# Rank-and-scatter kernel: twelve tiles of row copies from register loops, even groups, ranks finished by batch, a ring of four groups, an early Pool drain

## Chip, cores, metric

One core of one Trainium2 chip. The metric is the device time of one execution in microseconds (us), measured on the chip; every figure of time is a median of several executions unless it is called a span. The span is what the profiler sees, from the first to the last instruction, and is 1 to 3 us shorter than the time.

## The reference

For each of 8 batches, 2048 rows of 2560 floats (10 KB a row) are put in the order of their scores:

```python
B, N, D = 8, 2048, 2560
order = np.argsort(scores, axis=1)
ranks = np.argsort(order, axis=1)
out[b_idx, ranks, :] = x
```

So 168 MB are read and 168 MB written, and a row's place is its rank.

## The kernel before

VectorE counts, for each row, how many scores of its batch are smaller. That gives ranks. The rows are then moved in two ways.

*Bulk.* Pool loads a group (256 rows, 128 partitions x 20 KB, or 128 rows x 10 KB) into one of eight buffers and then writes each tile of 128 rows with one indirect DMA, a "scatter", to the rows that the ranks name. All of this goes through one DMA queue, q0. A load is issued only when the scatters `LAG` groups back have landed:

```python
NBUF = 8; LAG = 2; G = 16
GROUPS = [(0, 1, range(B)), (P, 1, range(3))] + [(256 * i, 2, ()) for i in range(1, 8)]
...                                             # (first row, tiles, batches done by row copy)
for k in range(1, NBUF):
    load(pl, k, s_load[k])
for k, (b, g) in enumerate(BULK):
    i = k % NBUF
    if k >= LAG and k + NBUF - LAG < len(BULK):
        scatters_done(pl, k - LAG)              # 16 increments, one per DMA engine, for each scatter
        load(pl, k + NBUF - LAG, s_load[(k - LAG) % NBUF])
    ...                                         # wait for the load of k and for its ranks
    for j in range(GROUPS[g][1]):
        scatter(k, j, 0, P, rank_i, s_scat[i][j])   # (the SPLIT branch is never taken: SPLIT is empty)
```

*Row copies.* 11 of the 128 tiles go straight from `x` to `out` without a buffer, a row at a time, from the two hardware queues of SP (q1) and ACT (q10). The loop is unrolled: 704 DMAs on each.

```python
for n, (b, g, j, q) in enumerate(todo):
    line, name = ((sp, ENG.SP), (act, ENG.Activation))[n % 2]
    ...                                         # at = 16 destination addresses loaded in registers
    for i in range(G):
        row = r + m * (G * q + i) + j
        line.eng.dma_start(
            out=out_bytes[bass.ds(at[i], ROW)],
            in_=x_bytes[b, row, :],
        ).then_inc(s_rows[line], 16)
```

At the end SP waits for the last scatters; Pool issues nothing after its last scatter.

## Time and profile before

| | before |
|---|---|
| time | 795.67 us (795.51 to 795.81, 3 runs) |
| span of the profiled run | 795.4 us |
| DMA, all 16 engines | busy in every slice, about 404 GB/s over the span |
| VectorE / PE / Pool busy | 411 / 33 / 148 us |

Read it from the DMA side: no compute engine is busy for more than about half of the span, and the DMA engines are full throughout. The page's line of busy times (us, share of the span, instructions):

```profile
PE 33.3 (4%) x155; PEld 27.2 (3%) x155; DVE 411.2 (52%) x1002; POOL 148.4 (19%) x186
```

The slices, queues and stretches are in the prediction, which works with them. The DMA row is a mean of 16 engines. Packet records carry a queue, a size and a duration.

### The profile page before, as it was taken

How to read it: one execution, taken by the hardware profiler on the slowest of the kernel's cores; microseconds unless marked ns; L12 is line 12 of the kernel's file. 1: busy time of each engine (PE TensorE's matmuls, PEld its weight loads, DVE VectorE, ACT ScalarE, POOL GpSimd, SP SyncE). 2: the span in 40 equal slices, each digit the busy share in tenths (PEclk: the TensorE clock that was granted, in tenths of full speed). 3: DMA queues.
4: the chain of work that ended last, by engine and by line, in shares of the span. 5: the costliest groups of instructions: out<-in, count | busy, mean ns of one | idle time of the engine just before them, and what ended most of it. 6: DMA issues, size and time to landing. Idle time of an engine off the chain costs nothing.

```text
span 795.4 us, 4586 instructions
## 1 busy us (share of the span) xinstructions
PE 33.3 (4%) x155; PEld 27.2 (3%) x155; DVE 411.2 (52%) x1002; POOL 148.4 (19%) x186
## 2 busy tenths in 40 slices
PE   3002010020020100200000000000000000000000
PEld 3001010010010100100000000000000000000000
DVE  6999999999999999999994000000000000000000
POOL 3102121212121212022111212122121212111600
PEclk9555555555555555555555555555555555555555
DMA  8999999999999999999999999999999999999994
GB/s 364 431 402 365 424 415 425 417 422 417 425 417 418 347 420 422 422 367 420 421 420 423 397 397 421 420 419 380 420 411 423 420 386 407 401 431 426 390 428 193
DMA packets 70737, 321.57 MB, mean 404 GB/s; under 512 B 25384, under 2 KB 47912, under 8 KB 47912
## 3 DMA queue, kind: packets, MB, share of 16 engines
q0 software_dynamic: 25488, 304.10, 91.3%
q1 hardware_dynamic: 22688, 9.94, 4.9%
q10 hardware_dynamic: 22528, 7.25, 3.9%
q14 instruction: 32, 0.26, 0.1%
q8 instruction: 1, 0.02, 0.0%
HBM read 167.84 MB, written 167.77 MB: 422 GB/s over the span
## 4 chain that ended last, share of the span: by engine, by line
DVE 47%; DMA 40%; issue 4%; POOL 3%; PE 1%; POOLq 0%; SPq 0%
DVE trash L258 41%; DMA out_dram<-x,rank_i 38%; DVE s_all L235 2%; DMA x<-in_x_dram 2%; POOL out_dram L361 2%; DVE rank L284 1%; DVE rank L290 1%; DVE rank_i L307 1%; POOL x L122 1%; DMA s_in<-in_scores_dram 0%; PE ps_all L190 0%; PE ps_col L169 0%; DVE rows_i L220 0%; POOLq L28 0%; DVE s_col L177 0%
## 5 line engine op out<-in xcount | busy, mean ns | idle before, releaser
L258 DVE TENSOR_SCALAR_CACHE_REDUCE trash<-s_all,s_col 128x1792 bf16<-128x1792 f32 (+9 forms) x248 | 315.3, 1306 | 0.3
L122 POOL DMA_DIRECT2D x<-in_x_dram x60 | 33.8, 565 | 545.8 <-DMA out_dram<-x,rank_i 376.5
L361 POOL DMA_INDIRECT out_dram<-x,rank_i x117 | 112.8, 964 | 59.0 <-issue 35.3
L258 DVE SCALAR_TENSOR_TENSOR trash<-s_all,s_col,mask 128x256 bf16<-128x256 f32 (+1 forms) x128 | 59.0, 461 | 0.0
L190 PE MATMUL ps_all<-ident,s_col 128*128 128x128 f32 x128 | 27.2, 399 | 247.4 <-DVE s_all L235 247.0
L190 PEld LDWEIGHTS ps_all<-ident,s_col 128*128 128x128 f32 x128 | 24.4, 213 | 249.4 <-DVE s_all L235 249.0
L235 DVE COPY s_all<-ps_all 128x512 f32<-128x512 f32 x32 | 20.1, 683 | 1.8 <-PE ps_all L190 1.5
L258 DVE DVE_READ_ACCUMULATOR trash<-s_all,s_col 128x1 f32 x248 | 19.9, 80 | 0.0
L290 DVE TENSOR_TENSOR rank<-rank,acc 128x2 f32<-128x2 f32 (+1 forms) x72 | 11.5, 160 | 2.5
L284 DVE TENSOR_TENSOR rank<-acc,acc 128x2 f32<-128x2 f32 (+1 forms) x72 | 11.5, 160 | 2.5
L307 DVE CAST rank_i<-rank 128x2 int32<-128x2 f32 (+1 forms) x61 | 10.7, 176 | 1.8
L258 DVE DVE_READ_ACCUMULATOR trash<-s_all,s_col,mask 128x1 f32 x128 | 10.2, 80 | 0.0
L300 PE MATMUL ps_row<-ident,rank 128*1 128x128 f32 x11 | 4.1, 372 | 101.3 <-DVE rank L290 92.7
L300 PEld LDWEIGHTS ps_row<-ident,rank 128*1 128x1 f32 x11 | 0.9, 79 | 105.0 <-DVE rank L290 95.5
L220 DVE TENSOR_SCALAR rows_i<-ps_row 1x128 int32<-1x128 f32 x11 | 3.0, 272 | 0.0
L177 DVE COPY s_col<-ps_col 128x128 f32<-128x128 f32 x1 | 0.3, 292 | 4.8 <-PE ps_col L169 4.8
L169 PE MATMUL ps_col<-ident,s_in 8*128 8x8 f32 x16 | 2.0, 261 | 4.0 <-DMA s_in<-in_scores_dram 4.0
L169 PEld LDWEIGHTS ps_col<-ident,s_in 8*128 8x128 f32 x16 | 1.9, 211 | 4.0 <-DMA s_in<-in_scores_dram 4.0
L150 POOL TENSOR_SCALAR_AFFINE_SELECT mask<-mask 128x256 f32<-128x256 f32 x2 | 0.8, 398 | 0.0
L162 DVE MEMSET acc<- 128x128 f32 x1 | 0.2, 165 | 1.1 <-SPq L98 1.1
L133 POOL MEMSET mask<- 128x512 f32 x1 | 0.5, 525 | 0.0
L132 POOL MEMSET ident<- 128x128 f32 x1 | 0.2, 204 | 0.5 <-SPq L98 0.5
(5 smaller groups left out, 0.7 us busy)
## 6 DMA issues: line engine op xcount, KB each, us to landing
x<-in_x_dram POOLq DMA_DIRECT2D x55, 2560.0 KB, 19.2
out_dram<-in_x_dram SPq DMA_DIRECT2D x704, 10.0 KB
out_dram<-in_x_dram ACTq DMA_DIRECT2D x704, 10.0 KB
x<-in_x_dram POOLq DMA_DIRECT2D x5, 1280.0 KB, 16.7
x<-in_x_dram SPq DMA_DIRECT2D x1, 2560.0 KB, 13.4
out_dram<-x,rank_i POOLq DMA_INDIRECT x117, 23.5
s_in<-in_scores_dram SPq DMA_DIRECT2D x1, 64.0 KB
```

Source lines behind the costliest of these rows:

```text
L122: line.eng.dma_start(out=xb[k % NBUF][:, :m * D], in_=x[b, r:r + P * m, :].rearrange("(p j) d -> p (j d)", j=m),).then_inc(sem, 16)
L150: nc.gpsimd.affine_select(out=part, in_=part, pattern=[[0, MMAX], [-1, P]], compare_op=OP.is_ge, fill=0.0, base=-half, channel_multiplier=1,)
L169: nc.tensor.transpose(out=ps_col[:, B * c:B * (c + 1)], in_=s_in[:, r + j:r + m * P:m], identity=ident[:B, :B],)
L190: nc.tensor.transpose(out=ps_all[:, P * c:P * (c + 1)], in_=s_col[:, c, b:b + 1].to_broadcast([P, P]), identity=ident[:],)
L220: nc.vector.tensor_scalar(out=rows_i[DIRECT.index((b, g))][:m, :], in0=ps_row[:m, :P], scalar1=float(b * N), scalar2=float(ROW), op0=OP.ad ...
L235: nc.vector.tensor_copy(out=s_all[:, 512 * q:512 * (q + 1)], in_=ps_all[:, 512 * q:512 * (q + 1)],)
L258: how.pop("do")(out=trash[i][:, :P * (hi_c - lo_c)], in0=s_all[:, P * lo_c:P * hi_c], accum_out=acc[which][:, col:col + 1], **how,)
L284: nc.vector.tensor_tensor(out=rank[:, cols], in0=acc[0][:, cols], in1=acc[1][:, cols], op=OP.add)
L290: nc.vector.tensor_tensor(out=rank[:, cols], in0=rank[:, cols], in1=acc[2][:, cols], op=OP.add)
L300: nc.tensor.transpose(out=ps_row[:m, :P], in_=rank[:, cols], identity=ident[:])
L307: nc.vector.tensor_copy(out=rank_i[:, cols], in_=rank[:, cols])
L361: nc.gpsimd.indirect_dma_start(out=out_flat, out_offset=bass.IndirectOffsetOnAxis(ap=index[:hi - lo, col:col + 1], axis=0), in_=xb[k % NBU ...
```

## The change

The intent: (1) even groups, so that every load and every group is two tiles; the first 256 rows of batches 0 to 5 are row copies, 12 tiles instead of 11; (2) the row copies as register loops, six per queue, 16 rows a pass, so that the code is short; (3) ranks of a batch finished together, fewer small VectorE instructions; (4) a ring in which a load waits for scatters four groups back instead of two; (5) a Pool drain after its last scatter, so that the runtime's own drain at the end finds nothing to do.

```diff
-    GROUPS = [(0, 1, range(B)), (P, 1, range(3))] + [(256 * i, 2, ()) for i in range(1, 8)]
+    GROUPS = [(256 * i, 2) for i in range(8)]
+    DIRECT = range(6)
...
-    LAG = 2
+    LAG = 4
...                                  # the ranks: the same counting operations, one add/add/cast
...                                  # for a batch (batch 0 in four steps) instead of one per group
+        for b in DIRECT:
+            for h, (line, name) in enumerate(((sp, ENG.SP), (act, ENG.Activation))):
+                line.after(dve, t_rows[b])
+                half = WIDE // 2
+                with line.eng.Fori(0, half // G) as q:
+                    _, at = nc.values_load_multi_w_load_instructions(
+                        rows_i[b][:, bass.ds(half * h + q * G, G)], ...
+                    for i in range(G):
+                        row = b * N + GROUPS[0][0] + half * h + i
+                        line.eng.dma_start(
+                            out=out_bytes[bass.ds(at[i], ROW)],
+                            in_=x_bytes[bass.ds(q * (G * ROW) + row * ROW, ROW)],
+                        ).then_inc(s_rows[line], 16)
...                                  # the unused SPLIT branch, rank_t, s_last go
             for j in range(GROUPS[g][1]):
+                scatter(k, j)
+        nc.gpsimd.drain()
```

## The prediction

> **What bounds the kernel now.** I read the page first (busy lines, slices, queues), then the same measures in stretches, then the packet records of the trace. Slices and queues of the page:
>
> ```profile
> DMA  8999999999999999999999999999999999999994
> GB/s 364 431 402 365 424 415 425 417 422 417 425 417 418 347 420 422 422 367 420 421 420 423 397 397 421 420 419 380 420 411 423 420 386 407 401 431 426 390 428 193
> ...
> q0 software_dynamic: 25488, 304.10, 91.3%
> q1 hardware_dynamic: 22688, 9.94, 4.9%
> q10 hardware_dynamic: 22528, 7.25, 3.9%
> q14 instruction: 32, 0.26, 0.1%
> ```
>
> The 16 DMA engines are full from the first slice to the last; the shares add up to 100%. VectorE is busy 411 us, all before 426 us, Pool 148 us. So only three things can move the time: work taken off the DMA engines, stretches in which they are busy but slow, and the two ends. The GB/s row shows the slow stretches: mostly about 420, but 347, 367, 380 now and then. The stretches:
>
> ```profile
> 75.00:259.00 184.00, 12.76 (x53) 10.22 (x53) 180.84 (x441) 32.38 (x39) 0.51 1.02 419
> 264.00:274.00 10.00, 2.18 (x10) 2.18 (x11) 9.83 (x20) 2.07 (x3) 0.50 1.05 292
> 339.00:349.00 10.00, 0.00 (x0) 0.00 (x0) 9.79 (x27) 2.49 (x3) 0.50 1.05 334
> 544.00:554.00 10.00, 0.00 (x0) 0.00 (x0) 0.00 (x0) 2.48 (x3) 0.50 1.02 350
> 734.00:744.00 10.00, 0.00 (x0) 0.00 (x0) 0.00 (x0) 6.93 (x8) 0.50 0.99 361
> 744.00:784.00 40.00, 0.00 (x0) 0.00 (x0) 0.00 (x0) 6.01 (x7) 0.50 1.00 425
> 784.00:791.00 7.00, 0.00 (x0) 0.00 (x0) 0.00 (x0) 0.00 (x0) 0.50 0.08 34
> ```
>
> The last two columns are DMA share and GB/s. 184 us run evenly at 419; then come dips of some 10 us with the engines as busy but at 292 to 388. The last line is the tail: one engine of 16 still works, alone, for about 6 us.
>
> The packet records say what the dips are. A 20 KB load packet takes 761 ns (median), a 10 KB scatter packet 385, a 640 B piece of a row copy 32 plus 9 for its completion. At these medians all packets add to (15616 x 385 + 7168 x 761 + 22528 x 41 + 2832 x 9) / 16 = 776 us per engine; the records add to 797. The 20 us between are load packets of up to 2200 ns (13 us) and row pieces (5 us), nearly all inside the dips. In the dips row pieces run at twice their usual rate per q0 packet.
>
> When do they come? Once at the start (50 to 75 us, where the first scatters follow eight loads). None from 75 to 259 us, batches 1 and 2, whose bulk groups are all two tiles. From batch 3 on each batch has one bulk group of a single tile (10 KB load packets, one scatter instead of two), and from 264 us there is a dip after nearly each such load and another where its lone scatter comes up (339, 444, 464, 544, 569, 644, 669, 734). I take the single-tile groups as the cause; the correlation is all I have.
>
> **What the skill says.** (1) "DMA: Bandwidth & Descriptors", section "Queues, rings and completion order": an engine round-robins between its queues at packet granularity. The trace agrees: from 75 to 259 us an engine took 384 q0 packets and 192 rows on each hardware queue, and a row is two packets. (2) Same page, "Where 436 GB/s comes from": a fabric ceiling of 435 GB/s. The pure scatter stretch has 425, the mix 419: nothing more is to be had there. (3) "Runtime: NRT & Kernel Launch", "Instruction fetch mechanics": instructions are streamed in 16 KiB blocks, and a taken branch outside the two-page window stalls on a fetch. The trace shows 32 packets of 8 KB on q14, about 0.31 us each; no loop is in this kernel, so it cannot show the stall.
>
> **The change, part by part.**
>
> *Twelve tiles instead of eleven by row copy.* Bulk costs (761/2 + 385)/16 = 47.6 ns of the 16 engines per row, a row copy 41. So 128 rows save 0.8 us.
>
> *All bulk groups two tiles.* The steady stretch repeats every 13.1 us per group of two tiles (load starts at 121.2, 134.3, 147.4). A period has 8 + 16 data and 3 completion packets of q0 per engine, 27, hence 27 row copies beside them. After the change there are 58 bulk groups: 58 x 13.1 = 760 us, with room for 58 x 27 = 1566 rows; 1536 are wanted. The row copies fit, with 2% to spare. The thirty missing rows give back 1.2 us. That is 758.6. The dips belonging to single-tile groups should go: 12 us by the GB/s missing in the eight stretches against 420 (3.05 + 2.05 + 0.9 + 0.9 + 1.7 + 1.2 + 1.0 + 1.4), some 17 by the spacing of the load starts there over 13.1 us per pair; the difference is row pieces served ahead, which are work too.
>
> *Register loops.* SP and ACT issue 704 rows each:
>
> ```profile
> L341 SPq MOVE out_dram<-in_x_dram x704: 29/29/38, 24.3 to 690.1; - x176
> L341 SPq DMA_DIRECT2D out_dram<-in_x_dram x704: 517/548/2704, 24.3 to 690.2; - x176
> L330 SPq TENSOR_LOAD <-rows_i x44: 967/1654/3367, 23.1 to 676.6; - x44
> ```
>
> Unhindered, one row takes 0.63 us (median spacing at the start), plus 1.75/16 = 0.11 for the load of 16 registers. After, 768 rows have from about 20 us to about 775: 0.98 us each. A source address that depends on the loop register costs perhaps two or three more register instructions of some 65 ns (the distance from MOVE to DMA), and the branch 0.03 per row: 0.63 + 0.11 + 0.16 + 0.03 = 0.93. It fits, barely. The code shrinks by about 2 x 1400 instructions of 64 bytes, some 20 of the 32 fetch packets, 6 us. That would matter little spread over 16 engines (0.4 us), but one engine ends 6 us behind the other fifteen, and 32 x 0.31 = 10 us of fetches on one engine would explain that. I credit 3 of the 6.
>
> *Ranks by batch.* Batch b's scatters wait for all its ranks: about 59 us for batch 0, 107 for batch 1 (48 us each, some 5 less than the 52 before). Pool then has three groups of batch 0 scattering and L and S packets for 46 us behind; by this estimate the ring runs dry at about 126, so 107 is early enough. Later batches are further ahead. Hidden; VectorE's saving is hidden too.
>
> *Four groups in the ring.* The wait before a load is on scatters four groups back, not two. The idle of Pool (376 us on scatters) is not on the path, since the ring never ran dry before. Worth 0, perhaps a longer pure scatter phase at the start.
>
> *Drain.* At the end the runtime's drain of Pool stands alone:
>
> ```profile
> L420 POOLq DRAIN  x3: 46/72/3015, 791.6 to 795.1; - x3
> ```
>
> 3.0 us after the last landing at 790.9. A drain put after Pool's last scatter (753 us) runs beside 38 us of transfers. If the later one then is short, 2.9 us are won; I count 2.4.
>
> *Sum.* Start 3 (the first slice's 364 GB/s against 430) + 758.6 + start dip 3 + 3 unexplained + late engine 3 + end 2 = 773. The 3 unexplained come from the same sum for the kernel before: 3 + 58.5 x 13.1 - 171 missing rows x 0.041 + 6 late engine + 4.4 end = 773; with 17 of dips and 2.3 at the start, 792 of 795.4. The other way: 795.7 - 12.2 dips - 3 late engine - 2.4 drain - 0.8 = 777. I take 775.
>
> **Rivals.** (a) The dips stay: they come from something else, such as engines drifting into step, and the deeper ring changes nothing or spreads them. For it: one dip at the start has no single-tile group. Against it: 184 us without one. Then 795.7 - 6 = 788 to 790. (b) Row issue becomes the bound: at 1.05 us per row SP would end at 20 + 806, so 826 us; loops straddling a fetch block would add to it. For it: only 2% of room; a straddling loop or a fourth register instruction is enough. Against it: my count of 0.93, and some thirty rows of buffer in each hardware queue (31 issued in the first 20 us while about 16 rows had been served). A milder form, rows ending a few us after the scatters, is likely; 2 us for it lie between my two sums. (c) Rank starvation at batch 1: an idle stretch near 110 us, at most some 10 us. (d) The drain's 3 us recur at the end: 778.
>
> **Range and chances.** The limit of 2% is 779.8. Most mixtures of half-credits lie between 768 and 789. Dips gone and rows fitting: about two chances in three, below the limit. Dips staying: about a quarter. Rows over time or starvation beyond 2%: one in twenty.
>
> **What would show it.** Right: the GB/s row even at 415 to 425 after some 90 us, the load packets' sum close to their medians, row copies ending within 15 us of the last scatter, fewer than 15 q14 packets, the last engine within 3 us of the others, and a final Pool drain under 0.1 us. Wrong: dips persisting in batches 3 to 7 with no single-tile groups; SP's and ACT's row spacing above 0.98 us with q0 empty at the end; a hole near 110 us; a final drain still of 3 us.

## The result, and the profile after

| | before | after |
|---|---|---|
| time, same rounds | 795.59 us (794.1 to 795.81, 4 runs) | 793.43 us (793.15 to 793.65, 4 runs) |
| ratio | | 0.9977 [0.9959, 0.9994]: the same |
| span of the profiled run | 795.4 | 791.4 |

A ratio here and below is the mean time of one kernel's fast runs over the mean of the other's in the same rounds, so it is not quite the ratio of the quoted medians; the bracket is its 95% interval.

The predicted 775.0 is missed by 18 us, and the range by 4. Yet most signs that the prediction had named for "right" are there. Slices and queues of the changed kernel's page:

```profile
DMA  8999999999999999999999999999999999999960
GB/s 366 423 407 416 425 416 423 418 425 415 427 414 425 415 424 416 425 420 422 419 419 421 420 422 420 422 418 423 418 424 419 422 419 423 418 425 418 417 252 19
...
q0 software_dynamic: 24912, 301.48, 89.5%
q1 hardware_dynamic: 24736, 10.60, 4.9%
q10 hardware_dynamic: 24576, 7.91, 4.0%
q14 instruction: 14, 0.11, 0.0%
```

From the fourth slice to the 38th it stays between 414 and 427 GB/s: the dips are gone. Fetch packets fell from 32 to 14. But look at the end: DMA 9, 6, 0 instead of 9, 9, 4. The same measures in stretches (width in us after the window; the last two columns are DMA share and GB/s), the dips' windows first:

```profile
75.00:259.00 184.00, 11.47 (x54) 10.17 (x54) 177.08 (x359) 0.00 (x0) 34.98 (x42) 0.51 1.02 420
264.00:274.00 10.00, 4.00 (x18) 3.52 (x18) 8.26 (x16) 0.00 (x0) 0.00 (x0) 0.67 1.02 419
339.00:349.00 10.00, 0.00 (x0) 0.00 (x0) 9.89 (x23) 0.00 (x0) 2.56 (x3) 0.50 1.05 432
544.00:554.00 10.00, 0.00 (x0) 0.00 (x0) 0.00 (x0) 0.00 (x0) 2.48 (x3) 0.50 1.02 418
764.00:786.00 22.00, 0.00 (x0) 0.00 (x0) 0.00 (x0) 0.00 (x0) 0.00 (x0) 0.50 0.07 30
```

The windows that had 292, 334 and 350 GB/s now have 419, 432 and 418. The last line is the news: for 22 us, 764 to 786 us, the DMA share is 0.07, which is one engine of sixteen, and 30 GB/s. Before, the engines were full until 784 and one worked alone for some 6 us. **Fifteen engines now finish 20 us earlier; the sixteenth finishes 4 us earlier between these two profiled runs, and it is the one that sets the end.**

The packet records show the same. Their clock runs some 10.7 us ahead of the span's. Each scatter ends with a 4-byte completion on every engine. The last completions of q0 come, in the kernel before, at 795.7, 798.7 and 801.8 us; in the changed one at 777.1, 777.6, 780.5, 783.9, 787.2, 790.6, 793.9 and 797.3 us. One per 3.3 us is what a single engine needs for its eight 10 KB packets of a scatter beside row pieces: one engine is seven scatters behind; before, it was two.

*What the slow engine does.* I followed its chain of q0 packets back from the last completion: at each step to a packet of the right size that ended just before the next began. The records have no engine number, so single links can be wrong; the sums are what I use. After the first 70 us, against the other fifteen:

| changed kernel | last engine | others | times | us |
|---|---|---|---|---|
| scatter packets, 10 KB, mean ns | 402.0 | 385.8 | 918 | 14.9 |
| load packets, 20 KB, mean ns | 764.1 | 761.3 | 400 | 1.1 |
| gaps in which row pieces are served, us | 50.5 | 43.5 | | 7.0 |
| fetch packets | 2 | 0 | | 0.6 |
| sum | | | | 23.6 |

The other engines are done at about 774, it at 797.3: the sum is the lag.

A check made afterwards divides the same sum more sharply. In this trace nearly every packet starts 3 or 4 ns before the end of the packet before it on its engine, whatever the queue, and the order of sizes in each queue is known. With both, all sixteen chains can be followed at once, and they hardly mix. After 70 us the last engine then has 919 scatter packets of 406.9 ns on average, 562 of them over 400 ns; the others have 385.4 on average, and at most 5 over 400 on any one. Its loads take 764.6 ns against 761.2, its gaps 47.0 us against 45.3. So about 20 of the 23 us are stretched scatter packets. The single chains used in the table above, and in the tables and means below, mix in some packets of other engines, so their "last" means for scatters are on the low side.

Spread over sixteen engines the work would have ended at (15 x 774 + 797.3) / 16 = 775.5 instead of 797.3, 22 us earlier: 772 us of time, an estimate from these records. So the sum in the prediction, which treats the sixteen as one pool, was close to right for the pool.

*The row copies fit.* SP's instructions of the loop (duration in ns min/median/max, then the first and last start):

```profile
L311 SPq MOVE out_dram<-in_x_dram x1536: 29/29/128, 19.8 to 759.6; - x192
L311 SPq DMA_DIRECT2D out_dram<-in_x_dram x768: 447/521/2196, 19.9 to 759.6; - x192
L311 SPq ALU_OP  x728: 32/33/55, 19.7 to 759.4; - x182
```

A register source address costs one ALU_OP of 33 ns and a second MOVE of 29 ns, 62 ns a row; the median spacing of rows inside a pass of 16 rose from 0.646 to 0.742 us. With the register load and the step to the next pass, the fastest passes take 0.84 to 0.89 us a row, below the 0.98 that the time allows.

*The drain.* The early one, and the one at the end:

```profile
L350 POOLq DRAIN  x1: 37592/37592/37592, 752.9 to 752.9; - x1
```

```profile
L379 POOLq DRAIN  x3: 34/47/72, 790.7 to 791.2; - x3
```

The longest drain at the end is 0.07 us instead of 3.0. But the early one lasts until 790.5, 3.8 us after the last landing, so the end still comes 4.7 us after the last landing (before: 4.4).

### The profile page after: what moved, and what is told of

Its sections match the earlier page's. It is cut to its first block, busy times and chain, and to the rows that moved or that the text cites. A ratio compares the mean times of both kernels' runs of the same rounds, so it can differ in the third digit from the quotient of the medians.

```text
span 791.4 us, 7991 instructions
## 1 busy us (share of the span) xinstructions
PE 30.9 (4%) x156; PEld 27.6 (3%) x156; DVE 398.3 (50%) x809; ACT 0.0 (0%) x1; POOL 146.2 (18%) x182
## 4 chain that ended last, share of the span: by engine, by line
DVE 43%; another core or an unknown queue 30%; POOL 8%; DMA 6%; issue 6%; PE 3%; POOLq 0%; SPq 0%
DVE trash L207 41%; POOL out_dram L328 6%; DMA x<-in_x_dram 6%; PE ps_all L180 2%; POOL x L112 2%; DVE s_all L279 1%; PE ps_row L254 0%; DMA s_in<-in_scores_dram 0%; PE ps_col L159 0%; DVE rank_i L245 0%; DVE rank L239 0%; DVE rank L233 0%; POOLq L350 0%; POOLq L28 0%
## 5 line engine op out<-in xcount | busy, mean ns | idle before, releaser
L207 DVE TENSOR_SCALAR_CACHE_REDUCE trash<-s_all,s_col 128x1792 bf16<-128x1792 f32 (+7 forms) x240 | 315.2, 1348 | 4.6
L112 POOL DMA_DIRECT2D x<-in_x_dram x57 | 32.1, 566 | 462.2 <-DMA out_dram<-x,rank_i 441.1
L207 DVE SCALAR_TENSOR_TENSOR trash<-s_all,s_col,mask 128x256 bf16<-128x256 f32 x128 | 61.6, 481 | 0.0
L207 DVE DVE_READ_ACCUMULATOR trash<-s_all,s_col,mask 128x1 f32 x128 | 10.7, 83 | 0.0
L264 DVE TENSOR_SCALAR rows_i<-ps_row 1x256 int32<-1x256 f32 x6 | 2.5, 411 | 4.1 <-PE ps_row L254 4.1
L245 DVE CAST rank_i<-rank 128x16 int32<-128x16 f32 (+3 forms) x11 | 2.0, 180 | 0.4
L239 DVE TENSOR_TENSOR rank<-rank,acc 128x16 f32<-128x16 f32 (+3 forms) x11 | 1.9, 170 | 0.4
L233 DVE TENSOR_TENSOR rank<-acc,acc 128x16 f32<-128x16 f32 (+3 forms) x11 | 1.9, 170 | 0.4
```

What stands on the lines that cost most here:

```text
L112: line.eng.dma_start(out=xb[k % NBUF][:, :m * D], in_=x[b, r:r + P * m, :].rearrange("(p j) d -> p (j d)", j=m),).then_inc(sem, 16)
L207: do(out=trash[i][:, :P * (hi_c - lo_c)], in0=s_all[:, P * lo_c:P * hi_c], accum_out=acc[i][:, col:col + 1], **how,)
L233: nc.vector.tensor_tensor(out=rank[:, cols], in0=acc[0][:, cols], in1=acc[1][:, cols], op=OP.add)
L239: nc.vector.tensor_tensor(out=rank[:, cols], in0=rank[:, cols], in1=acc[2][:, cols], op=OP.add)
L245: nc.vector.tensor_copy(out=rank_i[:, cols], in_=rank[:, cols])
L264: nc.vector.tensor_scalar(out=rows_i[b][:].rearrange("o (p j) -> o p j", p=P), in0=ps_row[:1, :WIDE].rearrange("o (j p) -> o p j", p=P), s ...
```

## The experiments

Theory A: the dips of the kernel before were the fifteen engines held back to the slow one by the short ring; the deeper ring lets them go, and the end is the slow engine's own chain. The code allows it: with `LAG` = 2, the load that follows group k-1's scatters in the queue is issued only after group k-2's scatters have landed on all sixteen engines. A fast engine that has finished group k-1 has nothing of q0 until then; it can be ahead by about one group (13.1 us less the issue), or half of that when the group is a single tile. With `LAG` = 4 it is three groups. Rival B is the prediction's: the dips belong to the single-tile groups themselves. Further rivals concern the slow engine: instruction fetches, the drain, the row copies.

### 1. The ring alone, in the kernel before

```diff
-    LAG = 2
+    LAG = 4
```

> The kernel before with the four-group ring alone; its single-tile groups stay. Theory A (one DMA engine of 16 is behind; a short ring holds the other fifteen back to it, which is what the dips are; its own work sets the end): the dips go, that engine ends 15 us or more behind the others, and the time stays within 1% of before (788 to 798). Rival B (the dips belong to single-tile groups, as I predicted): the dips at 264 us and after stay, and the last engine stays about 6 us behind.

Measured: 794.21 us (794.06 to 794.54) against 795.45; ratio 0.9984 [0.9967, 1.0001]. Slices:

```profile
DMA  8999999999999999999999999999999999999960
GB/s 363 432 399 415 423 416 423 417 425 414 425 417 425 418 418 423 419 420 420 419 424 418 419 420 420 426 421 417 422 417 426 421 417 422 417 426 432 427 283 20
```

All single-tile groups are still there and the dips are not. Load packets beyond their median fell from 13.4 to 2.0 us per engine. The other engines are done at about 777 (record clock), the last at 798.7: a lag of 22 us, made with one number. B falls and A stands: one changed number gives the whole picture of the changed kernel.

### 2. The short ring, in the changed kernel

```diff
-    LAG = 4
+    LAG = 2
```

> The changed kernel with two groups in the ring instead of four. Theory A: dips come back although no group has a single tile, the last engine is only some 6 us behind, and the time is about the changed kernel's, 790 to 797. Rival B: no dips, an even 420 GB/s, the lag stays above 15 us.

Measured: 792.54 us (792.39 to 792.95) against 795.45; 0.9965 [0.9948, 0.9982]. Slices:

```profile
DMA  8999999999999999999999999999999999999992
GB/s 365 426 406 399 424 416 426 415 424 418 422 416 427 416 394 417 417 404 415 415 404 410 422 419 415 418 385 426 414 415 416 416 404 410 415 420 404 421 420 80
```

The dips come back (394, 404, 404, 385, 404) with no single-tile group in the kernel, but shallower than before (347, 367, 380). Excess of the loads: 9.7 us, against 13.4 before. That fits the length of a group: single-tile groups were not the cause, but made the short ring shorter in time. The fifteen end at about 785, the last at 796.2: a lag of 11 us, where some 6 had been expected, and no later end than with the deep ring. The deep ring is worth nothing here.

### 3. No row copies

```diff
-    DIRECT = range(6)
+    DIRECT = range(0)
```

> The changed kernel without any row copy: 64 bulk groups. Theory A1 (the slow engine's scatter packets are stretched only while row copies run: 402 ns on it against 386 on the others): all scatter packets 385 ns, all engines end within 2 us, 64 x 12.2 + 8 = 788 to 791 us, so no slower than the changed kernel. Rival C (that engine is slow on scatters anyway): it ends 64 x 16 x 17 ns = 17 us behind the others and the time is 803 to 808.

Measured: 798.36 us (798.13 to 798.42) against 795.45; 1.0036 [1.0019, 1.0053]. Slices:

```profile
DMA  8999999999999999999999999999999999999994
GB/s 364 432 411 429 418 434 426 423 428 422 431 427 421 432 427 429 433 429 429 432 429 432 430 430 429 431 431 432 427 433 431 427 436 429 429 432 430 428 430 203
```

The time missed what I expected by 8 us: I had added the start and end wrongly, and some lag stays. The mechanism came out: the scatter packets of the last engine are 385.7 ns on average, the others' 385.2; 2 of 1007 are over 400. The stretching that made most of the lag is gone with the row copies. The last engine still ends at 801.6, 1.5 to 7 us behind the others (794.3 to 800.1), where 2 us had been expected, from a few long loads (771.6 against 765.4 on average) and 4 fetches.

### 4. Row copies on ten engines, first attempt

```diff
+                        if i % 3 == 0:
+                            to, of = (v.rearrange("(a b) -> a b", a=10) for v in (to, of))
```

> The changed kernel with every third row copy (6 of 16) cut into 10 pieces of 1024 bytes in place of 16 of 640, so that 576 rows use only ten engines. Theory A with the slow engine among the six left out: it is relieved of 576 x 38 ns = 22 us, the ten get 9 us more, and the end moves from 797 to about 783 in the packet records: 777 to 783 us. If the slow engine is among the ten: 798 to 806 us. If what it does is not the bound: within 1% of 793.

Measured: 793.31 us (792.61 to 793.57); 0.9970 [0.9954, 0.9987]. The edit did nothing: every row is still 16 packets of 640 B, 12288 on each queue. As a repeat of the changed kernel it shows the same lag (others 775, last 797.2; 401.5 against 386.0 ns). Inconclusive for its question.

### 5. Less bulk on one engine

Two bulk groups loaded and scattered with 120 of 128 partitions, meant to leave an engine free, their 32 left-over rows by row copy:

```diff
+    PART = {(5, 1): 120, (7, 1): 120}
...
-                out=xb[k % NBUF][:, :m * D],
+                out=xb[k % NBUF][:PART.get((b, g), P), :m * D],
```

> The changed kernel, but two of its 58 bulk groups move only 120 of 128 partitions; the 32 rows left over go by row copy. The Trainium skill says that a software-queue transfer of that height may leave out the last engine. Theory A, if the slow engine is the last one and it is left out: it is relieved of 2 x (8 x 0.76 + 16 x 0.40) = 25 us and pays 32 x 0.05 back, ends with the others at about 775 in the packet records, and the time is 769 to 776 us. If another engine is the slow one, or the transfers spread over all 16: 790 to 796 us and a lag of 20 us as now.

Measured: 824.47 us (820.29 to 825.6) against 795.35; 1.0346 [1.0317, 1.0376]. The rule that this expectation rests on is in the section of the Trainium skill that is quoted under 12 to 15. A misfire: the transfers of 120 partitions have 48 completion packets more than full ones (2816 in all instead of 2768; 24 for each of the six such transfers instead of 16, if shared evenly), and for the last 25 us of the scatters only about four packets run at once. How the transfers were spread over the engines was not established. Nothing follows for the slow engine.

### 6. Without the early drain

```diff
-        nc.gpsimd.drain()
```

> The changed kernel without the Pool drain. The trace of the changed kernel shows that drain running 37.6 us, until 3 us after the last landing. If the drain merely waits for the landings and then takes the same 3 us: ratio to before as the changed kernel's, 0.9977 within 0.0015. If it saves the final drain, as I predicted: 2.9 us (0.0036) slower than that.

Measured: 797.16 us (796.91 to 797.63) against 795.35; 1.0023 [1.0006, 1.0039]. The drain at the end:

```profile
L378 POOLq DRAIN  x3: 46/72/6847, 787.7 to 794.9; - x3
```

Two outcomes had been named, no difference or 2.9 us; it is the second. The drain is worth about 0.0046 x 795 = 3.7 us in the changed kernel (from the two ratios to before). Without it the runtime's drain takes 6.85 us, where it took 3.0 in the kernel before and 3.2 with `LAG` = 4 there. Why it is longer in the changed kernel stays open.

### 7. The loops unrolled

```diff
-                with line.eng.Fori(0, half // G) as q:
+                for q in range(half // G):
```

> The changed kernel with its row loops unrolled. Theory A: fetches go from 14 to about 37, a few of them on the slow engine (9 were on it in the kernel before): at most 3 us slower, ratio 0.997 to 1.002. My prediction's idea that fetches make the laggard: its lag grows from 22 us by 6 us and the time to 799.

Measured: 794.97 us (794.61 to 795.46) against 795.35; 0.9995 [0.9978, 1.0012]. About 1.5 us slower than with loops; the last landing is 1.1 us later, the lag about 1 us longer. Fetches are a small part of the lag, not its main cause.

### 8. Half the row copies

```diff
-    DIRECT = range(6)
+    DIRECT = range(3)
```

> The changed kernel with 6 tiles by row copy in place of 12. Theory A1 (row copies stretch the slow engine's scatters while they run, some 52 ns per row on that engine against 48 for a bulk row): fifteen engines end at about 785 in the packet records, 11 us later than now, the slow engine about 12 us behind them, and the time hardly moves: 792 to 798 us. If row copies were worth on the engine that ends last what they are on the others (9 ns a row): 768 rows cost 7 us, 800 us.

Measured: 792.46 us (792.35 to 792.66) against 795.35; 0.9962 [0.9946, 0.9979]. Slices:

```profile
DMA  8999999999999999999999999999999999999992
GB/s 367 425 405 416 427 413 425 414 424 417 424 416 424 417 424 417 425 414 425 418 428 434 426 433 430 424 433 426 431 433 428 435 429 429 433 426 431 429 429 90
```

In the first half, with row copies, 420 GB/s, in the second 430. From 100 to 300 us 227 of 3951 scatter packets (of all engines) are over 390 ns; from 500 to 700 us, with the same loads and scatters and no row copy, none of 4254. Half the row copies were taken away, and the time is no longer: on the engine that ends last, a row copy costs no less than bulk. Beside bulk's 47.6 ns per row and engine, its row piece costs 41 ns, and the stretching and the longer gaps add (14.9 + 7.0) us / 1536 = 14 ns, 55 in all. By this estimate 768 rows fewer save 6 us there; 1 us is measured, so it is rough. For the fifteen others row copies are a gain, which nobody sees.

### 9 and 10. Row copies on fifteen engines

```diff
+                        cuts = ((0, 10200), (10200, 40)) if i % 4 == 0 else ((0, ROW),)
```

(9 with five tile pairs; 10 with every row cut and three.)

> The changed kernel with 10 tiles by row copy, and every fourth row copied as 10200 + 40 bytes: 10200 is not divisible by 16, so the piece should go to 15 engines (680 bytes each), the first fifteen. The slow engine carried no piece of the eight-partition score load at the start, so it is in the upper half; if it is the last one, 320 rows less relieve it by 320 x 0.05 = 16 us while the others gain 5: the end of the packet records moves from about 797 to 781, the time to 776 to 782 us. If it is another engine: 793 to 800 us. Packets of 680 bytes: 15 x 320 = 4800 if the cut works.

> Six tiles by row copy, every row of them as 10200 + 40 bytes. If the slow engine's scatters are stretched by its own row pieces (and it gets none now): no engine shows scatter packets above 386 ns on average, and another set of engines ends last, at about 796. If the issue of row copies stretches them whatever engines they run on: the engine's scatters stay near 400 ns while rows run, though it ends before the others. Time 790 to 800 us either way.

Measured: 844.24 us (841.04 to 845.13) against 795.3, 1.06 [1.0576, 1.0624]; and 899.51 us (2 runs), 1.1308 [1.1279, 1.1337]. The cut works (4800 packets of 680 B, 15 to a row), but the 40-byte remainders go out in 4-byte pieces, and with them scatter packets rise to 399 and 427.5 ns on average and loads to 780 and 809. Inconclusive: the remainder costs more than what was to be measured. The expectation of run 9 puts the slow engine in the upper half of the sixteen, from the start of its chain and the rule quoted under 12 to 15. Runs 12 and 14 contradict that; single links of such a chain can be wrong, as said above.

### 11. The drain alone, in the kernel before

```diff
+        nc.gpsimd.drain()
```

> The kernel before with the Pool drain after its last scatter and nothing else. As I predicted, 3 us off the end: ratio 0.996. As the changed kernel's trace suggests (the early drain lasts until 3 us after the last landing): ratio 1.000 within 0.0015.

Measured: 793.67 us (793.17 to 794.54) against 795.3; 0.9976 [0.9959, 0.9992]. The early drain and those at the end:

```profile
L392 POOLq DRAIN  x1: 41202/41202/41202, 750.6 to 750.6; - x1
...
L421 POOLq DRAIN  x3: 34/47/72, 791.9 to 792.4; - x3
```

One line gains as much as the whole change (0.9976 and 0.9977).

### 12 to 15. Which engine is it?

Transfers cut into ten or five equal pieces. The section "Why a DMA increments its semaphore by 16 and not by 1" of the Trainium skill's page "DMA: Bandwidth & Descriptors" says that a hardware-queue DMA of k pieces uses the lowest-numbered k engines. If the slow engine is not among them, it is relieved and the end comes earlier; if it is, later. In 12 and 13 a row is two transfers of 10 x 512 B, in 14 and 15 two of 5 x 1024 B (12: 3 rows of 16, 14: 2 of 16; 13 and 15: all):

```diff
+                        if i in (0, 5, 10):
+                            to, of = (v.rearrange("(a t c) -> t a c", t=2, c=512) for v in (to, of))
+                            cuts = [(to[t], of[t]) for t in range(2)]
```

> The changed kernel with 10 tiles by row copy, 3 rows of 16 (240) each copied by two transfers of 10 pieces of 512 bytes, which use ten engines only. Theory A, if the slow engine is not among the ten: it is relieved of 240 x 0.05 = 12 us, the ten get 240 x 0.029 = 7 us; the end of the packet records is 783 to 786 in place of 797, the time 779 to 783 us. If it is among them: 800 to 806. If two transfers per row stretch scatters as the 40-byte pieces did: over 810.

> Six tiles by row copy, every row by two transfers of 10 pieces of 512 bytes. If an engine's scatters are stretched by its own row pieces: the six engines without pieces have scatter packets of 385 to 386 ns on average and end about 30 us before the ten. If by the issue of row copies on any engine: one of the six still has about 400 ns. The ten end at about 807, the time is 800 to 810 us.

> The changed kernel with 10 tiles by row copy, 2 rows of 16 (160) each copied by two transfers of 5 pieces of 1024 bytes, on five engines only. Theory A, if the slow engine is not among the five: relieved of 160 x 0.05 = 8 us, it ends at 789 in the packet records; the five get 160 x 0.07 = 11 us and end at 787; time 784 to 788 us, below both kernels. If it is among the five: 804 to 810.

> Four tiles by row copy, every row by two transfers of 5 pieces of 1024 bytes. Own pieces: eleven engines without pieces have scatters of 385 ns, and if the slow engine is one of them no packet lies above 395 ns outside the five. Issue anywhere: some 200 of 3900 scatter packets in 200 us lie above 390 ns, on one engine, as in the changed kernel (215). Issue costs some 1.2 us per transfer, so 512 a queue take 650 us and do not set the end; the five get 512 x 112 ns = 57 us against 48 of bulk work saved, the time is 795 to 815 us.

*12, rows_low:* 799.4 us (799.14 to 799.74) against 794.78; 1.0057 [1.004, 1.0074]. Its last engine ends at 803.4, later than without the cut (797.3), and its chain has 512-byte pieces in its gaps. Its scatters: 397.1 ns against 385.6.

*14, rows_five:* 802.65 us (802.0 to 803.42) against 795.08; 1.0097 [1.008, 1.0114]. 160 rows in five pieces put 320 pieces of 46 + 9 ns on each of five engines instead of 160 of 41: 11 us more by these durations. At 785 us (record clock) five engines work, at 793 one, and it ends at 805.7: 8 us later than in the changed kernel, where 784 to 788 us of time had been expected if it were outside the five. The time lies just under the 804 to 810 expected if it is inside. In 238 of the gaps of its chain a 1024-byte piece starts, where chance gives some 60. So it is one of the five. Following all sixteen chains at once agrees: from 300 to 340 us five engines carry 17 or 18 of the 1024-byte pieces each and the others none, and the engine whose scatters are stretched (40 of 48 over 390 ns, at most 1 on any other) is one of the five. The trace shows that there are five, not that they are the lowest-numbered.

*13, all_low* (1 run, 898.63 us) was meant for the stretching and became a run of something else: SP still issues at 894 us. The issue of a row transfer:

```profile
L318 SPq DMA_DIRECT2D out_dram<-in_x_dram x768: 3/769/1213, 19.7 to 893.5; - x192
```

A transfer of ten pieces takes the sequencer 0.77 us, one of sixteen 0.52. The row issue became the bound, the prediction's rival (b). It cannot say whose row pieces matter, because the slow engine is among the ten. *15, all_five* (1 run, 838.7 us, expected 795 to 815) missed too: all row work is on five engines, these fall behind and hold the ring for the rest (load packets 819 ns on average), with GB/s down to 378 in places. That fits theory A's mechanism, with five slow engines in place of one. From 100 to 140 us the eleven engines without row pieces have no scatter packet over 390 ns, and one of the five has 28 of 48; but the slow engine is one of the five, so this does not say whose pieces matter.

The table sums up what bears on theory A (record clock; means in ns, after the first 70 us; "others" are the fifteen):

| kernel | LAG | row tiles | others done | last done | scatters last / others | loads, others | time us |
|---|---|---|---|---|---|---|---|
| before | 2 | 11 | 795.7 | 801.8 | 397.1 / 385.4 | 793.1 | 795.6 |
| before_lag4 | 4 | 11 | about 777 | 798.7 | 398.1 / 385.6 | 761.8 | 794.2 |
| after | 4 | 12 | about 775 | 797.3 | 402.0 / 385.8 | 761.3 | 793.4 |
| after_lag2 | 2 | 12 | about 785 | 796.2 | 401.5 / 385.4 | 782.9 | 792.5 |
| six_tiles | 4 | 6 | about 785 | 796.1 | 393.2 / 385.3 | 762.3 | 792.5 |
| no_rows | 4 | 0 | 794 to 800 | 801.6 | 385.7 / 385.2 | 765.4 | 798.4 |

"Others done" moves by 20 us, "last done" by 6, and the time follows the last. No version is clearly faster than both kernels: the two at 792.5 have intervals that overlap with the changed kernel's.

### A look at the kept traces: own row pieces, or their issue?

No run was made for this; the ends of the row copies in four traces answer a part of it. Times are in the record clock; stretched means over 390 ns.

- *Not the issue.* In six_tiles the last row transfer is issued at 388.2 us, while pieces are still queued. From then to 405 us the slow engine has 21 of 24 scatters stretched.
- *Not its own pieces alone.* Its row queues are behind those of the others, so at the end it serves row pieces alone, and then nothing is stretched. In six_tiles the others' last pieces come at 409 to 414.5 us; from 411.6 to 421.5 us none of its 16 scatters is stretched. In before_lag4 it serves 33 pieces alone from 719 to 736 us (19 scatters, all 385 ns), in before 54 from 711 to 738 (32 scatters, 385 to 388 ns), in the changed kernel 52 after 777.7 us (46 scatters, 385 ns).

So its scatters stretch while other engines serve row pieces as well. Why, and why on this engine alone, is not shown.

## Why the prediction was wrong, point by point

**The step that failed** is "I take the single-tile groups as the cause" of the dips, with "12 us" to "17" of gain for their going, and beside it "Four groups in the ring ... Worth 0" and "one engine ends 6 us behind the other fifteen ... I credit 3 of the 6". The dips did go, and they went from the ring (run 1), not from the groups. They were the fifteen engines waiting for the sixteenth, so removing them shortened only the fifteen. In place of a lag of 3 us there was one of 23, and the 12 to 17 us were paid into it. All three terms come of one assumption: that sixteen engines, all "9", are one pool, and that a slow stretch of the mean is a slow stretch of whoever ends last. The warning was in view: one engine ended 6 us behind although the program gives all the same work. I named fetches as its cause; run 7 shows about 1 us for them.

**The correlation was real.** The dips followed single-tile groups because these shorten what two groups last; run 2 still has dips without them, shallower. That the group length is the link is argued from the code and the sizes of the dips, not shown by a run of its own. Why loads lengthen in a dip (793 ns on average on the fifteen) is not shown either.

**More row copies "save 0.8 us".** Wrong in kind for the engine that counts: halving them did not lengthen the time (run 8). The 41 ns per row left out that this engine's scatters stretch beside row copies.

**Row issue.** The count of 0.93 us a row was somewhat high (0.84 to 0.89 for the fastest passes), the conclusion right: they fit. The rival of a row-bound kernel appeared only in run 13.

**Loops.** Fetch packets 14, "fewer than 15" as predicted; worth about 1.5 us (run 7) instead of 3. The step from one pass to the next took 2.2 to 2.7 us in the first passes, where it took 1.7 to 2.1 unrolled; no longer stall at the branches was seen.

**Ranks by batch.** Hidden, as predicted: no hole near 110 us, 420 GB/s from 75 to 259.

**Drain.** Predicted 2.4. Alone in the kernel before it gives 0.0024 x 795 = 1.9 us (run 11), in the changed kernel 3.7 (run 6). The final drain under 0.1 us came true; the early one ends 3.8 us after the last landing, which the prediction had taken as hidden.

**The sum.** Of 795.6 - 793.4 = 2.2 us, the drain alone accounts for about as much by run 11. The other parts net to about nothing at the end: the last engine's end moved 4 us between the two profiled runs, but the one of before was a long one (span 795.4; its executions in the later runs have spans of 792.6 to 794.8), and the tail from the last landing to the span's end did not shrink.

**What stays open.** Which of the five engines is slow, and why its scatters stretch while it and others serve row pieces. No experiment relieved that one engine of row pieces alone (4, 5, 9, 10 misfired, 12 to 15 showed that it is among the lower ones). The leftover lag without row copies is not explained in full, nor is the 6.85 us of run 6. And in before_lag4, with no row piece left, 77 of 288 scatter packets from 770 to 780 us are over 390 ns. As 64 of them fall in 5 us, in which one engine serves some 13, at least five engines are concerned: another stretching, without a known cause.

## What to carry to other kernels

Before crediting the end of a slow stretch on sixteen DMA engines, ask which engine ends last and whether the stretch lies on its chain: here 20 us came off fifteen engines and 4 off the one that mattered. A ring whose loads wait for all sixteen completions ties the fast engines to the slowest, so dips in the mean can be waiting; a deeper ring then moves the idle time to the end and wins nothing. The tail of the DMA row, where the share falls to 1/16, is the first thing to size, and a one-line early drain can be worth as much as a rewrite.

## What the Trainium skill lacked or had wrong

- "DMA: Bandwidth & Descriptors", section "Latency and other measured facts", says that engines 7 and 15 are usually slower, with software-queue descriptor fetches as a best guess and hardware queues free of it. Here one engine's scatters are stretched while hardware-queue row copies run on it and on others: 406.9 ns on average against 385.4 with them, 385.7 against 385.2 without (run 3); and within one run, over the same loads and scatters, 227 of 3951 packets are stretched beside row copies and none of 4254 after them (run 8). By the same page's rule of the lowest k engines it is among the first five (run 14), so neither 7 nor 15. The records have no engine number, so this rests on that rule.
- The same page says how an engine shares its queues, and that a DMA needs all 16 increments, but not what follows for a ring: with a lag of two groups, one slow engine holds back the fifteen (load packets of 793 ns on average instead of 762), with four they run 22 us ahead (run 1).
- The same page, section "Why a DMA increments its semaphore by 16 and not by 1", says that with fewer than 16 pieces the sequencer writes the rest itself, but gives no price for this chip. Here a ten-piece transfer takes SP 0.77 us to issue (run 13), a sixteen-piece one 0.52 (changed kernel). Their access patterns differ too, so how much of this is the writing is not shown.
- The same section says that with software queues all 16 engines post the completion, whatever the shape. Here the six transfers of 120 partitions (two loads, four scatters) have 48 four-byte completion packets more than full ones: 24 each, if shared evenly, instead of 16 (run 5).
- "VectorE: DVE Perf Modes", section "The DRAIN you can't avoid", says that the runtime's drains take about 12 ns, constant, on all five engines. Here that is so for SP, ACT, VectorE and TensorE (7 to 10 ns), but Pool's longest one takes 3.0 us at the end before, 6.85 in run 6, 0.07 after an earlier drain. No page that was found says what a Pool drain costs after scatters.
